# Three of the seven MLP input blocks made on chip, and the causal mask moved into the scan, in a one-layer trunk kernel

## The chip, the cores and the metric

The kernel runs on one core of a Trainium2 chip. Time is device time of one execution in microseconds (us); lower is better. A core has a matrix engine (PE, whose weight loads PEld run beside it), three engines for element work (DVE, ACT, POOL) and a queue engine (SP) that issues loads; stores are issued from POOL's queue. PE works at one of two clocks, which the profile gives as a granted share: 1.0 or 0.5.

## The reference, cut to what matters

One layer, 2048 tokens, width 1024: stick-breaking attention (8 heads of 64), a gated convolution and a spatial gate share one projection; then an MLP of width 4096.

```
h   = rmsnorm(x) * (1 + scale_m) + shift_m
p   = h @ w_in                        # split into q, k, v, conv and gate columns
mix = concat[attention, conv, gate] @ w_out
x   = x + gate_m * mix
h   = rmsnorm(x) * (1 + scale_f) + shift_f
x   = x + gate_f * (relu(h @ w1)**2 @ w2)
out = rmsnorm(x)

# attention, z = q k^T / 8, mask = key < query (strict)
log_stay  = where(mask, log_sigmoid(-z), 0)
log_after = reverse_cumsum(log_stay) - log_stay
w   = where(mask, exp(log_sigmoid(z) + log_after), 0)
out = w @ v
```

## The kernel before

All matrix work is done on numbers split in two parts (`split`: a rounded part by an ACT cast at L127, the remainder by a DVE subtraction at L130), three matmuls for each product.

The program has these stages in time. **Phase 1** (0 to about 713 us) does both halves of 1024 tokens: normalise, project, attention, convolution and gate. Attention is 64 tasks (`attention`): each makes the scores z of two query blocks of 128 against 256 keys each, has them turned into weights by `weights` (three ACT functions, a DVE step, two DVE scans, a copy, a DVE subtraction, an ACT exponential), then transposes and multiplies by v. A matmul of a bf16 mask tile with a bf16 identity (L459) adds a large negative number to the scores that the causal mask forbids. **Output blocks** (713 to about 942) multiply the mix by w_out, first half and then second (the second from about 820); each tile of 512 columns is read from its bank `po` by DVE (`mo`, L769) and stored as rows `x`.

While the second half's output blocks run, the first half's MLP input is prepared in steps that the output loop calls two at a time (`prepare_input`, started by `bg.tick`): load two rows tiles, square sums on ACT (L207), four small DVE steps and two scalings (`x`, L987), transposes on PE into `pt` (L992), shift and scale on ACT into `hf` (L997), store to DRAM (`hd`). Then four passes load pairs of these tiles back (`a1`, `a2`) and DVE makes the sums S1 to S4 (L1011 to L1014), stored to DRAM (`hs`). **Up** (942 to 1600) is a seven-product scheme for the first MLP matrix: products with the key `ababcbc` accumulate in three banks (pa, pb, pc), 16 units for each half of the tokens. Its moving operands are seven blocks of the input, A11, S2, A12, S3, S1, A22, S4 (numbers 0 to 6), each loaded from DRAM by `input` and split into SBUF tiles (h0 to h7 or hx). The second half's input is prepared in the background of the first half's units in the same way. **Down** (1600 to 2216) is the second MLP matrix: its first operands `w` (from DRAM `ar`) and h0 to h7 are split during Up's last products, and its four accumulators py take over Up's banks; the third of them is pc's bank.

Every engine runs its instructions in the order of its queue; that order is fixed when the kernel is built. A load waits for one of six landing buffers, the tiles `hf`, `mo`, `xr` and `hs` share a pool of six.

Of the kernel before, what the change touches and what calls it, by code (L numbers as in the profile page):

```python
# [19 lines left out]
P = 128  # L20
D = 1024
# [63 lines left out]
def trunk(ctx: ExitStack, tc: tile.TileContext, x, c, ada_w, ada_b, norm_mix_g, norm_mlp_g,  # L85
# [224 lines left out]
    with ExitStack() as ph:  # L310
# [86 lines left out]
        identb = ac.tile([P, P], BF16, name="identb")  # L397
        mask = ac.tile([P, 256], BF16, name="mask")
# [4 lines left out]
        def mixer_constants():  # L403

            V.tensor_copy(identb, ident)
            m32 = etile("m32")[:, :256]
            GP.memset(m32, 0.0)
            GP.affine_select(out=m32[:, P:], in_=m32[:, P:], pattern=[[-1, P]],
                             compare_op=ALU.is_gt, fill=NEG, base=0, channel_multiplier=1)
            GP.memset(m32[:, 0:P], NEG)  # L410
            V.tensor_copy(mask, m32)
# [20 lines left out]
        def weights(e, z, lo, init, save):  # L432
# [5 lines left out]
            for a, b in lo:  # L438
                r = e[:, a:b][:, ::-1]
                V.tensor_tensor_scan(r, r, r, init, ALU.add, ALU.bypass)  # L440
            V.tensor_copy(save, e.rearrange("p (b k) -> p b k", b=len(lo))[:, :, 0])
            V.tensor_tensor(e, z, e, ALU.subtract)
            A.activation(e, e, AF.Exp)

        def attention(half, pair, j, gl, qp, qq, kk, vv, a_sb):
# [5 lines left out]
            last = None  # L451
            for b in range(2):
                o = (2 * qp + b) * P
                c0 = 256 * b if first and b == 0 else 256 * b + P
                zb = z[:, b * 256:(b + 1) * 256]
                with tc.issue_after(last.ins) if last is not None else nullcontext():
                    T.matmul(zb, lhsT=qq[:, 0, o:o + P], rhs=kk[:, o:o + 256], start=True, stop=False)
                    T.matmul(zb, lhsT=qq[:, 1, o:o + P], rhs=kk[:, o:o + 256], start=False, stop=False)
                    last = T.matmul(z[:, c0:(b + 1) * 256], lhsT=identb, rhs=mask[:, c0 - 256 * b:256],  # L459
                                    start=False, stop=True)  # L460
            e = etile()
            weights(e, z, ((0, 256), (256, G)), 0.0, carry[:, half, h, ib:ib + 2])
# [451 lines left out]
    class Up:  # L914
# [55 lines left out]

        def prepare_input(self, half):

            for g in range(NG):
                for tp in range(2):
                    xs = []
                    ss = sp.tile([P, 4], F32, name="ss", tag="ss")
                    for b in range(2):
                        t0 = (2 * tp + b) * P
                        t = landing("x")
                        load(out=t, in_=x1d[half * NG + g][t0:t0 + P, :])  # L980
                        xs.append(t)
                    yield
                    for b in range(2):
                        sum_squares(ss[:, b:b + 1], xs[b])
                    r = rstd_of(ss[:, 0:2], 2, 1.0 / D)
                    for b in range(2):
                        V.tensor_scalar_mul(xs[b], xs[b], r[:, b:b + 1])  # L987
                    yield
                    for k in range(0, KT, 2):
                        pt = bank("pt")  # L990
                        for m in range(4):
                            T.transpose(pt[:, m * P:(m + 1) * P],  # L992
                                        xs[m % 2][:, (k + m // 2) * P:(k + m // 2 + 1) * P], ident)
                        f = etile("hf")
                        for m in range(2):
                            sl = slice(m * UC, (m + 1) * UC)
                            A.activation(f[:, sl], pt[:, sl], AF.Identity,  # L997
                                         bias=SH_F[:, k + m:k + m + 1], scale=SC_F[:, k + m:k + m + 1])
# [41 lines left out]
        def inputs_after(self, gl):  # L1040

            if gl == 0:
                bg.finish(self.coming)
                for i in (4, 5, 6, 0, 1):
                    self.input(0, i)
# [296 lines left out]
```

## Time and profile before

| | |
|---|---|
| median of 3 runs | 2219.91 us (2218.26 to 2220.62) |
| profiled execution | 2221.83 us |
| its span | 2220.1 us |
| mean granted PE clock | 0.985 |
| PE busy | 2129.2 us, 96% |
| DVE busy | 1445.0 us, 65% |
| ACT busy | 1013.7 us, 46% |

The span is the time between the first and last instruction of the profiled execution; 1.7 us lie around it. A busy PE is a PE with a matmul under way; matmuls overlap, so what one costs is read from the distance between two starts, not from its own duration.

### The profile page before, as it was taken

To read this page: it belongs to the slowest core of one execution; us is meant where nothing else is said; L and a number is where in the kernel's file an instruction comes from. 1 tells how busy PE (TensorE), PEld (TensorE's weight loads), DVE (VectorE), ACT (ScalarE), POOL (GpSimd) and SP (SyncE) were. 2 spreads that over 40 slices of the span, in tenths; PEclk is the share of its full clock that TensorE was granted. 3 is DMA by queue.
4 is the path that set the end of the run, shared out by engine and by line. 5 is a ranking of instruction groups with operands and counts; after the bars stand their busy time and mean duration, and the time that the engine had idled before them with its cause. 6 is when DMAs were issued, how large, how long until landed. Compare 5 with 4: busy or idle time off the path is not lost. (4 is left out here: it accounts for less than half of the span.)

```text
span 2220.1 us, 30066 instructions
## 1 busy us (share of the span) xinstructions
PE 2129.2 (96%) x11071; PEld 1797.7 (81%) x11071; DVE 1445.0 (65%) x2413; ACT 1013.7 (46%) x1718; POOL 332.0 (15%) x579
## 2 busy tenths in 40 slices
PE   7999999999999988899999999999999999999998
PEld 3887887888788988877888777878788888888886
DVE  4878868767768543776766777778743434347675
ACT  4645647645656234366444644444523323224432
POOL 0021211020211112223322132323200000000000
PEclk9999999999999999999999999999999999999999
DMA  8464544243435466967744687777854435437572
GB/s 304 134 207 115 163 142 131 68 140 88 117 121 162 135 224 233 327 225 244 280 156 154 225 280 256 253 237 248 308 188 153 159 120 165 143 126 231 199 241 86
DMA packets 223216, 415.37 MB, mean 187 GB/s; under 512 B 18400, under 2 KB 106416, under 8 KB 223056
## 3 DMA queue, kind: packets, MB, share of 16 engines
q1 hardware_dynamic: 177424, 264.28, 36.9%
q0 software_dynamic: 45504, 149.00, 19.3%
q8 instruction: 90, 1.47, 0.3%
q14 instruction: 70, 0.57, 0.1%
q10 hardware_dynamic: 128, 0.04, 0.0%
HBM read 262.18 MB, written 142.67 MB: 182 GB/s over the span
## 5 line engine op out<-in xcount | busy, mean ns | idle before, releaser
L1201 PE MATMUL py<-h,w 128*128 128x512 f32 x2688 | 610.7, 389 | 0.0
L1201 PEld LDWEIGHTS py<-h,w 128*128 128x128 f32 x2688 | 504.5, 188 | 105.8 <-issue 1.0
L130 DVE TENSOR_TENSOR w<-ar,w 128x1024 fp32r<-128x1024 f32 x112 | 137.1, 1224 | 263.7 <-ACT w L127 263.3
L127 ACT CAST w<-ar 128x1024 fp32r<-128x1024 f32 x112 | 118.0, 1054 | 370.4 <-PE py L1201 350.4
L127 ACT CAST w<-raw 128x512 fp32r<-128x512 f32 (+1 forms) x215 | 155.1, 736 | 131.4 <-PE pc L1089 48.9
L278 PE MATMUL po<-w,h 128*128 128x256 f32 x1536 | 195.0, 289 | 9.9 <-DVE mo L769 7.3
L130 DVE TENSOR_TENSOR w<-raw,w 128x512 fp32r<-128x512 f32 (+1 forms) x215 | 176.8, 834 | 37.9 <-ACT w L127 36.9
L278 PEld LDWEIGHTS po<-w,h 128*128 128x128 f32 x1536 | 191.4, 197 | 10.7 <-issue 10.0
L1089 PE MATMUL pc<-hx,w 128*128 128x512 f32 x768 | 193.2, 401 | 6.8 <-DVE hid L1063 6.8
L1089 PE MATMUL pa<-h,w 128*128 128x512 f32 x768 | 190.0, 396 | 7.8 <-ACT s L1056 7.8
L1089 PE MATMUL pb<-h,w 128*128 128x512 f32 x768 | 186.7, 391 | 3.6 <-DVE s L1058 3.6
L1089 PEld LDWEIGHTS pc<-hx,w 128*128 128x128 f32 x768 | 145.7, 190 | 42.6 <-DVE hid L1063 8.1
L1089 PEld LDWEIGHTS pa<-h,w 128*128 128x128 f32 x768 | 145.7, 191 | 42.4 <-ACT s L1056 11.2
L1089 PEld LDWEIGHTS pb<-h,w 128*128 128x128 f32 x768 | 143.8, 188 | 35.1 <-DVE s L1058 3.7
L269 PE MATMUL pc<-h,w 128*128 128x512 f32 x576 | 137.4, 394 | 0.0
L269 PEld LDWEIGHTS pc<-h,w 128*128 128x128 f32 x576 | 106.6, 188 | 21.3
L1064 ACT ACTIVATE hid<-hid 128x512 f32<-128x512 f32 x96 | 60.5, 630 | 124.2 <-DVE hid L1063 123.1
L278 PE MATMUL pv<-w,h 128*128 128x256 f32 x768 | 99.5, 285 | 0.0
L1300 POOL DMA_DIRECT2D out_dram<-y x24 | 13.0, 541 | 560.8 <-DVE y L1299 559.6
L1089 PE MATMUL pb<-hx,w 128*128 128x512 f32 x384 | 95.1, 396 | 1.2 <-DVE s L1058 1.2
L278 PEld LDWEIGHTS pv<-w,h 128*128 128x128 f32 x768 | 94.5, 191 | 0.1
L269 PE MATMUL pk<-h,w 128*128 128x512 f32 x384 | 94.1, 398 | 0.1
(215 smaller groups left out, 3285.3 us busy)
## 6 DMA issues: line engine op xcount, KB each, us to landing
ar<-ad SPq DMA_DIRECT2D x112, 512.0 KB, 3.9
ad<-hid POOLq DMA_DIRECT2D x128, 256.0 KB, 3.2
raw<-in_mlp_w_dram SPq DMA_DIRECT2D x62, 512.0 KB, 5.7
ad<-hsum POOLq DMA_DIRECT2D x96, 256.0 KB, 3.2
aw<-in_ada_w_dram SPq DMA_DIRECT2D x32, 512.0 KB, 4.5
f<-in_mlp_w_dram SPq DMA_DIRECT2D x32, 512.0 KB, 4.7
w2s<-f POOLq DMA_DIRECT2D x64, 256.0 KB, 2.9
w<-w2s SPq DMA_DIRECT2D x32, 512.0 KB, 4.5
```

The costliest lines, as they stand in the source:

```text
L127: A.copy(hi, src)
L130: V.tensor_tensor(lo, src, hi.bitcast(F32), ALU.subtract)
L269: T.matmul(ps, lhsT=w[k][:, a, c0:c0 + P], rhs=hT[k][:, b], start=n == 0, stop=n == 3 * KT - 1)
L278: T.matmul(ps, lhsT=hT[k][:, a, tb * P:(tb + 1) * P], rhs=w[k][:, b], start=n == 0, stop=n == 3 * KT - 1)
L1064: A.activation(t, t, AF.Relu)
L1089: T.matmul(ps[key], lhsT=w[:, a, k * P:(k + 1) * P], rhs=h[k // 2][:, b, k % 2], start=start and m == 0, stop=m == 11, skip_group_check=no ...
L1201: T.matmul(ps[tb], lhsT=self.a[q][:, a, u * G + tb * P:u * G + (tb + 1) * P], rhs=self.w[at, c][:, b, u], start=c == 0 and u == 0 and n == ...
L1300: (load if end else store)(out=out2[t0:t0 + P, sl], in_=y)
```

## The change

1. The mask matmuls go, and with them the rule that orders the two query blocks of a task. The scan gets a second operand `restart` (1, and 0 on the diagonal), with which the running sum is multiplied after each addition, so that it starts anew below the diagonal. After the subtraction, a DVE minimum with a tile `cap` (0 and a large negative number) is taken on the 2 x 128 columns of the keys of the query's own block.
2. The first half's S1, S2 and S3 are summed on DVE from the `hf` tiles while they are on chip, and split in place into the hx tiles (`prepare_first`, `sums_first`). A11, A12 and A22 still go through DRAM, and S4 is stored once summed. The half's DMAs: 12 stores of 256 KB into hd in place of 16, 4 into hs in place of 16, no reload of a1 and a2 (8 x 512 KB before), 8 loads of 512 KB of blocks in place of 14.
3. The steps before the transposes are called one by one, with more steps between (`rows_T`); this holds for both halves.
4. Blocks are loaded one step ahead of their splits; blocks 5 and 6 of the first half are split inside Up. The tiles hold other blocks: S2, S3 and S1 in hx, blocks 0, 2, 5 and 6 in h0 to h7. So Down's first operands are prepared after the products 0, 2, 5 and 6 of the last unit, each pair when its tiles are free (before: after 1 to 4).

```diff
-        def weights(e, z, lo, init, save):
+        def weights(e, z, lo, init, save, own=None):
...
                 r = e[:, a:b][:, ::-1]
-                V.tensor_tensor_scan(r, r, r, init, ALU.add, ALU.bypass)
+                if own is None:
+                    V.tensor_tensor_scan(r, r, r, init, ALU.add, ALU.bypass)
+                else:
+                    V.tensor_tensor_scan(r, r, restart[:, ::-1], init, ALU.add, ALU.mult)
...
             V.tensor_tensor(e, z, e, ALU.subtract)
+            if own is not None:
+                V.tensor_tensor(own, own, cap.unsqueeze(1).to_broadcast([P, 2, P]), ALU.min)
             A.activation(e, e, AF.Exp)
...
-                with tc.issue_after(last.ins) if last is not None else nullcontext():
-                    T.matmul(zb, lhsT=qq[:, 0, o:o + P], rhs=kk[:, o:o + 256], start=True, stop=False)
-                    T.matmul(zb, lhsT=qq[:, 1, o:o + P], rhs=kk[:, o:o + 256], start=False, stop=False)
-                    last = T.matmul(z[:, c0:(b + 1) * 256], lhsT=identb, rhs=mask[:, c0 - 256 * b:256],
-                                    start=False, stop=True)
+                for s in range(2):
+                    T.matmul(z[:, b * 256:(b + 1) * 256], lhsT=qq[:, s, o:o + P],
+                             rhs=kk[:, o:o + 256], start=s == 0, stop=s == 1)
...
+        def rows_T(self, half, g, tp, order, tile_):
...
+                load(out=t, in_=x1d[half * NG + g][t0:t0 + P, :])
+                xs.append(t)
+            yield None
+            yield None
+            for b in range(2):
+                sum_squares(ss[:, b:b + 1], xs[b])
+            yield None
+            r = rstd_of(ss[:, 0:2], 2, 1.0 / D)
+            for b in range(2):
+                V.tensor_scalar_mul(xs[b], xs[b], r[:, b:b + 1])
+            yield None
+            yield None
+            for k in order:
...
+        DIRECT = (1, 3, 4)
...
+        def prepare_first(self):
...
+            for tp in range(2):
+                kept = {}
+                for g in range(NG):
+                    order = (0, 4, 2, 6) if g else (0, 2, 4, 6)
+                    for got in self.rows_T(0, g, tp, order, lambda: self.out_tile("hf")):
+                        if got is not None:
+                            k, f = got
+                            kept[g, k] = f
+                            if g == 0 or k >= 4:
+                                self.put_rows(0, g, tp, k, f)
+                            if g == 1 and k >= 4:
+                                yield
+                                yield from self.sums_first(tp, k - 4, kept)
+                        yield
+
+        def sums_first(self, tp, k, kept):
+            a11, a12, a21, a22 = kept[0, k], kept[0, k + 4], kept[1, k], kept[1, k + 4]
+            s1, s2, s4 = (self.xp.tile([P, G], F32, name="s", tag="s", bufs=3) for _ in range(3))
+            V.tensor_tensor(s1, a21, a22, ALU.add)
+            V.tensor_tensor(a21, a11, a21, ALU.subtract)
+            V.tensor_tensor(s2, s1, a11, ALU.subtract)
+            V.tensor_tensor(s4, a12, s2, ALU.subtract)
...
+            store(out=hs[0][3][k:k + 2, :, cols_].rearrange("k p t -> p k t"),
+                  in_=s4.rearrange("p (k t) -> p k t", k=2))
+            for i, t in ((1, s2), (3, a21), (4, s1)):
+                yield
+                o = self.h[0][i][k // 2]
+                split(o[:, 0, :, cols_], o[:, 1, :, cols_], t.rearrange("p (k t) -> p k t", k=2), A)
...
-                if 0 < n - 7 * (NU - 1) <= 7:
-                    self.input(1, n - 7 * (NU - 1) - 1)
+                if n in (1, 3):
+                    if n == 1:
+                        self.loaded.append(self.input_load(0, 6))
+                    self.input_split(0, 5 + n // 2, self.loaded.pop(0))
+                at = n - 7 * (NU - 1)
+                if at == 0:
+                    self.loaded = [self.input_load(1, 0)]
+                if 0 < at <= 7:
+                    if at < 7:
+                        self.loaded.append(self.input_load(1, at))
+                    self.input_split(1, at - 1, self.loaded.pop(0))
                 last = n - self.N + 7
-                if 0 < last <= 4:
-                    down.weights(0, 2 * last - 2)
-                    down.weights(0, 2 * last - 1)
+                if last in (0, 2, 5, 6):
+                    c = 2 * (0, 2, 5, 6).index(last)
+                    down.weights(0, c)
+                    down.weights(0, c + 1)
```

On PE, the first attention task of the program stood like this before (z scores, kk and qq the keys and queries, identb and mask the bf16 tiles):

```order
L457 MATMUL z_1429<-kk_1352,qq_1312 128x256
L458 MATMUL z_1429<-kk_1352,qq_1312 128x256
L459 LDWEIGHTS identb_219
L459 MATMUL z_1429<-mask_220,identb_219 128x256
L457 MATMUL z_1429<-kk_1352,qq_1312 128x256
L458 MATMUL z_1429<-kk_1352,qq_1312 128x256
L459 LDWEIGHTS identb_219
L459 MATMUL z_1429<-mask_220,identb_219 128x128
L278 MATMUL pv_1446<-w_907,h4_552 128x256 x6
```

and stands like this in the changed kernel:

```order
L460 MATMUL z_1427<-kk_1350,qq_1310 128x256 x4
L278 MATMUL pv_1443<-w_905,h4_550 128x256 x6
```

Two mask matmuls and their weight loads are gone from each of the 64 tasks, and nothing has moved between the four score matmuls.

On PE, the first transposes of the preparation stood like this before (pt the transposes' banks, x the scaled rows, po a bank of the output blocks; po_9533 is the first bank of the second half's blocks):

```order
L278 MATMUL po_9533<-w_9384,h2_9312 128x256 x6
L278 MATMUL po_9533<-w_9384,h3_9313 128x256 x6
L992 MATMUL pt_9626<-ident_79,x_9569 128x128
L992 MATMUL pt_9642<-ident_79,x_9569 128x128
L992 MATMUL pt_9655<-ident_79,x_9569 128x128
L992 MATMUL pt_9626<-ident_79,x_9571 128x128
```

and stand like this in the changed kernel, where po_9467 is that first bank and po_9579 the second:

```order
L278 MATMUL po_9467<-w_9318,h3_9247 128x256 x6
L278 MATMUL po_9579<-w_9315,h0_9244 128x256 x6
L278 MATMUL po_9579<-w_9315,h1_9245 128x256 x6
L278 MATMUL po_9579<-w_9318,h2_9246 128x256 x6
L278 MATMUL po_9579<-w_9318,h3_9247 128x256 x6
L278 MATMUL po_9579<-w_9315,h0_9244 128x256 x6
L278 MATMUL po_9579<-w_9315,h1_9245 128x256 x5
L996 MATMUL pt_9604<-ident_79,x_9509 128x128
L996 MATMUL pt_9613<-ident_79,x_9509 128x128
L278 MATMUL po_9579<-w_9315,h1_9245 128x256
```

They stand 35 matmuls of the output blocks later.

On DVE, in the second half's output blocks, the sums of the first half's blocks stood like this before (hs the sums, a1 and a2 the tiles loaded back, mo the reading of an output bank po, w a split of Up's first weights):

```order
L1011 TENSOR_TENSOR hs_10196<-a1_10151,a2_10152 128x512
L1012 TENSOR_TENSOR hs_10197<-hs_10196,a1_10151 128x512
L1013 TENSOR_TENSOR hs_10198<-a1_10151 128x512
L1014 TENSOR_TENSOR hs_10199<-a2_10152,hs_10197 128x512
L130 TENSOR_TENSOR w_10307<-raw_10165,w_10307 128x1024
L130 TENSOR_TENSOR w_10310<-raw_10167,w_10310 128x1024
L1011 TENSOR_TENSOR hs_10236<-a1_10208,a2_10209 128x512
L1012 TENSOR_TENSOR hs_10237<-hs_10236,a1_10208 128x512
L1013 TENSOR_TENSOR hs_10238<-a1_10208 128x512
L1014 TENSOR_TENSOR hs_10239<-a2_10209,hs_10237 128x512
L769 TENSOR_TENSOR mo_10248<-po_10171,gate_bc_85 128x512
```

and the first of the four passes stands like this in the changed kernel (L771 and L773 are the lines of mo now, s the sums):

```order
L1044 TENSOR_TENSOR s_9788<-hf_9749,hf_9784 128x512
L1045 TENSOR_TENSOR hf_9749<-hf_9609,hf_9749 128x512
L1046 TENSOR_TENSOR s_9789<-s_9788,hf_9609 128x512
L771 TENSOR_TENSOR mo_9824<-po_9754,gate_bc_85 128x512
L1047 TENSOR_TENSOR s_9790<-hf_9651,s_9789 128x512
L130 TENSOR_TENSOR hx_9502<-s_9789,hx_9502 128x2x256
L130 TENSOR_TENSOR hx_9504<-hf_9749,hx_9504 128x2x256
L773 TENSOR_TENSOR mo_9824<-mo_9824,xr_9752 128x512
L130 TENSOR_TENSOR hx_9506<-s_9788,hx_9506 128x2x256
```

The last two passes before stood in one piece ahead of a reading of a bank; now readings stand between the sums of a pass, the sums read tiles that ACT made and not loaded ones, and three half-width splits follow each pass. Between the transposes and the scaling of the next rows, one place is different too: two splits of Up's weights stand ahead of the third scaling,

```order
L196 TENSOR_SCALAR v_9984<-ss_9947 128x2
L130 TENSOR_TENSOR w_9996<-raw_9830,w_9996 128x1024
L771 TENSOR_TENSOR mo_9980<-po_9920,gate_bc_85 128x512
L199 TENSOR_TENSOR t_9986<-r_9985 128x2
L130 TENSOR_TENSOR w_9999<-raw_9832,w_9999 128x1024
L773 TENSOR_TENSOR mo_9980<-mo_9980,xr_9918 128x512
L200 TENSOR_TENSOR t_9986<-t_9986,v_9984 128x2
L201 TENSOR_SCALAR t_9986<-t_9986 128x2
L202 TENSOR_TENSOR r_9985<-r_9985,t_9986 128x2
L990 TENSOR_SCALAR x_9948<-x_9948,r_9985 128x1024
```

where before they stood behind the last of them.

On DVE, at the end of Up, the reading of the last product's bank pc (the second `hid<-pc`) stood like this before (hid the activations, hsum their sums, room a piece of modulation work, w and h splits of Down's operands):

```order
L130 TENSOR_TENSOR h6_16083<-w2_16081,h6_16083 128x1024
L130 TENSOR_TENSOR h7_16088<-w2_16086,h7_16088 128x1024
L130 TENSOR_TENSOR w_16093<-ar_16091,w_16093 128x1024
L1063 TENSOR_TENSOR hid_16096<-pc_16068,s_16066 128x512
L1063 TENSOR_TENSOR hid_16121<-pb_15984,s_15982 128x512
L130 TENSOR_TENSOR w_16147<-ar_16145,w_16147 128x1024
L1070 TENSOR_TENSOR hsum_16125<-hid_16121,hid_16096 128x512
L365 TENSOR_SCALAR room_16166<-aw_16203,cact_160 128x512
L1070 TENSOR_TENSOR hsum_16128<-hsum_16125,hid_16040 128x512
L1125 TENSOR_TENSOR hid_16121<-hid_16040,hid_16121 128x512
L1063 TENSOR_TENSOR hid_16150<-pc_16068,s_16007 128x512
```

and stands like this in the changed kernel:

```order
L1132 TENSOR_TENSOR hid_15974<-pc_15956,s_15954 128x512
L130 TENSOR_TENSOR h4_16001<-w2_15999,h4_16001 128x1024
L1132 TENSOR_TENSOR hid_16009<-pb_15892,s_15890 128x512
L130 TENSOR_TENSOR h5_16006<-w2_16004,h5_16006 128x1024
L130 TENSOR_TENSOR w_16045<-ar_16043,w_16045 128x1024
L130 TENSOR_TENSOR h6_16035<-w2_16033,h6_16035 128x1024
L1139 TENSOR_TENSOR hsum_16013<-hid_16009,hid_15974 128x512
L130 TENSOR_TENSOR h7_16040<-w2_16038,h7_16040 128x1024
L1139 TENSOR_TENSOR hsum_16016<-hsum_16013,hid_15938 128x512
L1204 TENSOR_TENSOR hid_16009<-hid_15938,hid_16009 128x512
L1132 TENSOR_TENSOR hid_16048<-pc_15956,s_15905 128x512
```

Four splits (h4 to h7) have come to stand between the first reading of pc and the second. On ACT, the casts that belong to them stand in this order in the changed kernel:

```order
L127 CAST h5_16006<-w2_16004 128x1024
L127 CAST w_16045<-ar_16043 128x1024
L1133 ACTIVATE hid_16009<-hid_16009 128x512
L127 CAST h6_16035<-w2_16033 128x1024
L1134 ACTIVATE hid_16009<-hid_16009 128x512
L127 CAST h7_16040<-w2_16038 128x1024
L1133 ACTIVATE hid_16048<-hid_16048 128x512
```

The tiles h4 to h7 hold blocks 5 and 6 of Up now, so the cast of h5 can't start before the sixth of the last unit's seven products has ended, and that of h7 not before the seventh.

## Rows read from the trace of the kernel before

**Rows 1.** The page: busy time, share of the span and instructions of each engine.
```profile
PE 2129.2 (96%) x11071; PEld 1797.7 (81%) x11071; DVE 1445.0 (65%) x2413; ACT 1013.7 (46%) x1718; POOL 332.0 (15%) x579
```
**Rows 2.** Busy time by stage (start:end length, busy us of each engine, clock, DMA, GB/s).
```profile
0.00:713.00 713.00, 673.45 (x3964) 573.14 (x3964) 522.25 (x1029) 406.56 (x744) 97.42 (x167) 0.98 0.47 144
...
820.00:942.00 122.00, 103.11 (x803) 101.39 (x802) 63.32 (x102) 45.19 (x80) 30.83 (x47) 0.92 0.84 285
942.00:1250.00 308.00, 301.75 (x1333) 245.14 (x1332) 215.07 (x353) 164.50 (x299) 77.05 (x136) 0.99 0.58 205
1250.00:1600.00 350.00, 334.76 (x1421) 268.83 (x1420) 269.34 (x405) 172.18 (x283) 97.70 (x182) 0.99 0.77 265
```
**Rows 3.** What PE waited for from 820 to 945 (us, times, longest).
```profile
PE pt L992 <- DVE x L987: 11.1, 4, 4.7
PE po L278 <- DVE mo L769: 7.3, 1, 7.3
```
**Rows 4.** PE from 818 to 910 (start, us, work, [idle before <-releaser]).
```profile
826.75 2.79 PE L992 MATMUL pt<-ident,x 128*128 128x128 f32 x12 [4.67 <-DVE x L987]
...
839.40 0.43 PE L992 MATMUL pt<-ident,x 128*128 128x128 f32 x2 [2.66 <-DVE x L987]
...
850.65 0.30 PE L992 MATMUL pt<-ident,x 128*128 128x128 f32 x1 [3.51 <-DVE x L987]
...
868.58 29.05 PE L278 MATMUL po<-w,h 128*128 128x256 f32 x240 [0.26 <-ACT hf L997]
904.93 5.33 PE L278 MATMUL po<-w,h 128*128 128x256 f32 x24 [7.30 <-DVE mo L769]
```
**Rows 5.** DVE from 884 to 906.
```profile
900.96 0.69 DVE L1012 TENSOR_TENSOR hs<-hs,a 128x512 f32<-128x512 f32 x1 [1.37 <-DMA hs<-hs]
...
904.09 0.69 DVE L769 TENSOR_TENSOR mo<-po,gate_bc 128x512 f32<-128x512 f32 x1 [0.41 <-DMA hs<-hs]
```
**Rows 6.** Two short stretches, columns as in rows 2.
```profile
826.50:831.50 5.00, 4.75 (x22) 4.45 (x23) 2.06 (x4) 2.85 (x6) 1.68 (x3) 0.50 0.67 230
...
899.70:909.90 10.20, 4.97 (x23) 5.00 (x24) 7.08 (x10) 1.04 (x1) 3.61 (x6) 0.50 0.90 309
```
**Rows 7.** PE in one attention task, from 309.7 to 311.
```profile
310.10 0.36 PE L457 MATMUL z<-kk,qq 128*128 128x256 f32 x1
310.30 0.28 PE L458 MATMUL z<-kk,qq 128*128 128x256 f32 x1
310.43 0.23 PE L459 MATMUL z<-mask,identb 128*128 128x128 bf16 x1
310.46 0.36 PE L457 MATMUL z<-kk,qq 128*128 128x256 f32 x1
```
**Rows 8.** The mask matmuls as a group (count, busy us, mean ns).
```profile
L459 PE MATMUL z<-mask,identb 128*128 128x128 bf16 x120 | 27.6, 230 | 0.0
```
**Rows 9.** Groups of DVE in phase 1 (count, busy us, mean ns).
```profile
L440 DVE TENSOR_TENSOR_SCAN e<-e 128x256 f32<-128x256 f32 x122 | 77.8, 676 | 1.1
...
L442 DVE TENSOR_TENSOR e<-z,e 128x512 f32<-128x512 f32 x60 | 41.1, 686 | 1.4
...
L659 DVE TENSOR_TENSOR gu<-gu,mx 128x128 f32<-128x128 f32 x32 | 8.9, 278 | 0.1
```
**Rows 10.** What PE waited for from 945 to 1250.
```profile
PE pt L992 <- DVE x L987: 2.1, 3, 1.4
```
**Rows 11.** PE from 1594 to 1604: the last product of Up.
```profile
1597.11 3.06 PE L1089 MATMUL pc<-hx,w 128*128 128x512 f32 x12 [1.13 <-DVE hid L1063]
```
**Rows 12.** The page's groups: a split's two steps, and an activation.
```profile
L130 DVE TENSOR_TENSOR w<-ar,w 128x1024 fp32r<-128x1024 f32 x112 | 137.1, 1224 | 263.7 <-ACT w L127 263.3
L127 ACT CAST w<-ar 128x1024 fp32r<-128x1024 f32 x112 | 118.0, 1054 | 370.4 <-PE py L1201 350.4
...
L1064 ACT ACTIVATE hid<-hid 128x512 f32<-128x512 f32 x96 | 60.5, 630 | 124.2 <-DVE hid L1063 123.1
```
**Rows 13.** DVE from 1594 to 1606: the second reading of pc.
```profile
1601.81 0.68 DVE L1063 TENSOR_TENSOR hid<-pc,s 128x512 f32<-128x512 f32 x1
```

More of the change, by code (lines that the diff above doesn't have):

```diff
@@ L1 @@
-from contextlib import ExitStack, nullcontext
+from contextlib import ExitStack
 import concourse.bass as bass
@@ L395, in mod_rows @@
                 yield
-        identb = ac.tile([P, P], BF16, name="identb")
-        mask = ac.tile([P, 256], BF16, name="mask")
+        restart = ac.tile([P, 256], F32, name="restart")
+        cap = ac.tile([P, P], F32, name="cap")
         swT = ac.tile([P, 2, 4 * P], F32R, name="swT")
@@ new lines, in put_rows, with place @@
+        def put_rows(self, half, g, tp, k, f):
+            t0 = g * G + tp * UC
+            store(out=hd[half][k:k + 2, :, t0:t0 + UC].rearrange("k p t -> p k t"),
+                  in_=f.rearrange("p (k t) -> p k t", k=2))
+        DIRECT = (1, 3, 4)
+        def place(self, i):
+            if i in self.DIRECT:
+                n = 2 * self.DIRECT.index(i)
+                return [self.xp.tile([P, 2, 2, G], F32R, name="hx", tag=f"hx{n + j}")
+                        for j in range(2)]
+            n = 2 * (0, 2, 5, 6).index(i)
+            return [htile(n + j) for j in range(2)]
@@ new lines, in prepare_first @@
+        def prepare_first(self):
+            for i in self.DIRECT:
+                self.h[0][i] = self.place(i)
+            for tp in range(2):
[12 more added lines that the diff above has]
+                        yield
@@ L974, in prepare_input @@
                 for tp in range(2):
[L975 to L998, printed above, removed]
-                        t0 = g * G + tp * UC
-                        store(out=hd[half][k:k + 2, :, t0:t0 + UC].rearrange("k p t -> p k t"),
-                              in_=f.rearrange("p (k t) -> p k t", k=2))
+                    for got in self.rows_T(half, g, tp, range(0, KT, 2), lambda: etile("hf")):
+                        if got is not None:
+                            self.put_rows(half, g, tp, *got)
                         yield
@@ L1016, in prepare_input, with input_load @@
                     store(out=hs[half][j][k], in_=e[j])
-        def input(self, half, i):
-            tiles = []
+        def input_load(self, half, i):
+            raws = []
             for j in range(2):
@@ L1031, in input, with input_split, first_inputs @@
                 load(out=raw, in_=src.rearrange("k p t -> p k t"))
-                if i < 4:
-                    t = htile(2 * i + j)
-                else:
-                    t = self.xp.tile([P, 2, 2, G], F32R, name="hx", tag=f"hx{2 * i + j}")
-                split(t[:, 0], t[:, 1], raw, A)
-                tiles.append(t)
-            self.h[half][i] = tiles
+                raws.append(raw)
+            return raws
+        def input_split(self, half, i, raws):
+            tiles = self.h[half][i] = self.place(i)
+            for t, raw in zip(tiles, raws):
+                split(t[:, 0], t[:, 1], raw, A)
+        def first_inputs(self):
+            raws = self.input_load(0, 0)
+            yield
+            for i, after in ((0, 2), (2, 5)):
+                ahead = self.input_load(0, after)
+                for _ in range(3):
+                    yield
+                self.input_split(0, i, raws)
+                raws = ahead
+            self.loaded = [raws]
         def inputs_after(self, gl):
+            bg.finish(self.coming)
             if gl == 0:
-                bg.finish(self.coming)
-                for i in (4, 5, 6, 0, 1):
-                    self.input(0, i)
-            else:
-                for i in (2, 3):
-                    self.input(0, i)
+                self.coming = bg.now(self.first_inputs())
         def out_tile(self, name):
```

35 lines of the change are left out of this document (24 added, 11 removed).

## The prediction

> **What bounds the kernel now.** I read the page first, then busy time by stage, then PE's waits and timeline in the stages that the change touches, and last the other engines' timelines around the longest waits. PE is busy 96% of the span, DVE 65% [rows 1], so the kernel is as long as PE's work plus the stretches in which PE waits or runs at half clock. In phase 1 PE is idle for 713.0 - 673.45 = 39.6 us, spread over many short waits; in the second output stage for 122.0 - 103.1 = 18.9 us, with a mean granted clock of 0.92 where phase 1 has 0.98; in the two parts of Up for 6.3 and 15.2 us [rows 2]. So there are two things to win: PE work taken away, and the waits of the output stage.
>
> Nearly all of those 18.9 us are four waits [rows 3, 4]: three times the transposes of the preparation wait for the scaled rows (4.67, 2.66, 3.51 us), once the output matmuls wait 7.30 us for a bank to be read. The reading came late because it stands on DVE behind the sums hs, which wait for stores of earlier sums to free their tiles: at 900.96 and just before 904.09 the releaser is the store of hs [rows 5]. The DMA engines are 84% busy in this stage [rows 2]. After two of the waits the trace shows PE at half clock, from 826.5 to 831.5 and from 899.7 to 909.9, with 4.75 and 4.97 us of PE work in them [rows 6]; done at full clock that is half as long, so another 4.9 us were lost. Together the stage loses 23.8 us.
>
> **Masks.** In one attention task the first score matmul of the second block starts 0.36 us after that of the first [rows 7]. Plain matmuls of the same shape follow each other at 29.05 / 240 = 0.121 us [rows 4], so two of them should take 0.242, and the mask with its weight load takes 0.118. The group's mean duration, 230 ns [rows 8], would give 0.230, but those durations overlap: the distance counts. 64 tasks x 2 x 0.118 = -15.1 us. The Trainium skill ("TensorE: Matmul & The Clock Gate", section "Back-to-back issue gap") states about 81 ns per matmul for a sustained stream of pairs of weight load and 128-column matmul. By this figure the masks would be worth an estimated 10.4 us and the sum below -25; the distance of rows 7 speaks against it, and I go by the rows.
>
> What the change adds for it is 64 minimums on DVE. The trace has none of 256 columns of this form; DVE takes 0.278 us for 128 columns and 0.686 for 512 [rows 9], so on a line between them 0.41 us for 256, or 26 us of DVE in all. The bounds are the two rows, 18 to 44 us. DVE has 522 us of work in 713 [rows 2]; it will have 548 in some 700. The minimum also stands in each task's chain from scores to transposes, making it 0.4 us longer; PE has other tasks' matmuls in between. It costs nothing where that cover holds. It does not hold everywhere: PE's 39.6 us of waits in this stage are such places. Per task DVE goes from 8.2 to 8.6 us and PE from 10.5 to 10.3, so I let the waits grow by 3 us (bounds 0 and 10, the latter about 0.4 us for 24 of the 64 tasks). The scan's second operand is priced at nothing: the scan named two operands before, and at 0.676 us for 256 columns it takes 2.6 ns a column, where a subtraction that reads two tiles takes 0.686 for 512, or 1.3 ns [rows 9]; the reading isn't what limits it. Phase 1: -12 us, from -5 to -15.
>
> **Output stage.** The sums no longer wait for reloads or for stores of four tiles; they read tiles that ACT has just made, and of the sums S4 alone is stored; there are 16 of them as before. In MB, 4 hd and 12 hs stores of 256 KB, 8 reloads and 6 block loads of 512 KB go, about 11 MB of the 35 MB that 285 GB/s over 122 us make [rows 2]. The mechanism of the 7.30 us wait is therefore gone, and with it its 2.5 us of half clock: -9.8. The new order shows three DVE readings of banks between the sums and splits of the first pass where before two passes and two wide splits stood ahead of one. Nothing as long as 7 us can gather on DVE without DMA waits: four sums (0.69 each) and three half splits are 4.8 us, and a reading stands inside them.
>
> The first transposes stand 35 output matmuls later: 35 x 0.121 = 4.2 us of the 4.67 us wait are filled, and the 2.4 us of half clock behind it go too. The second and third wait (2.66 and 3.51) come from the same steps, where ACT's square sums and DVE's scaling were asked for one step ahead of the transposes; there are two more steps there now. But two wide splits stand ahead of the third scaling: 2 x 1.22 us of DVE [rows 12], fed by two casts of 1.05. That leaves an estimated 1 to 2 us of wait at this place; about 0.5 at the first, 0 to 2 at the fourth. I keep 4 us of the 23.8 in all: -20 us. Bounds: -12 (the 7.30 with its clock and 2 us more), -24 (all).
>
> **Up.** The same longer steps serve the second half's rows: three waits of 2.1 us in total [rows 10], of which I take 2 off: -2 (0 to -4). Blocks 5 and 6 are split within the first unit, their loads a step earlier; the first wait there stays about as it was: 0 +- 1. Loading the second half's blocks a step ahead does not change the order of splits on ACT and DVE: 0 +- 4, the latter a fourth of the 15.2 us of waits in that part.
>
> **Up to Down: a new wait.** Down's third accumulator uses pc's bank, so PE can start it only when DVE has read the last product. Call T the end of that product. The first two accumulators take 12 matmuls, as many as the last product, which ran 3.06 us from its first start to its last end [rows 11]; starts alone are a little closer, so PE wants the bank at about T + 2.8. In the new order that reading stands behind four splits, whose casts must wait for Up's last products because they write into their tiles. ACT from the end of the sixth product (T - 2.8): h5, w, an activation, h6, an activation, h7, or 4 x 1.05 + 2 x 0.63 = 5.5 us [rows 12], so T + 2.7. DVE behind it: a split of 1.22, two sums and the reading, each 0.69 or 0.68 [rows 9, 13]: T + 2.7 + 1.22 + 3 x 0.69 = T + 6.0, and one more combination at 0.69 if the sums weren't done before it: no more than T + 6.7. PE waits 3.2 to 3.9 us, and may lose up to 1.7 at half clock behind it, as after the waits of 3.5 us. Before, PE waited 1.13 us ahead of the last product [rows 11], and the last reading at 1601.81 [rows 13] came in time. That 1.13 wait hung on a split's operand from DRAM and may go or stay. I take +4, bounds 0 and +10 (a late load of `ar` would stand ahead of all of it).
>
> **Sum.** -12 - 20 - 2 + 4 = -30 us from the profiled 2221.83 gives 2192. The median of the runs is 1.9 us lower; measured against it, the same sum would be 2190. I say 2191.
>
> **The rivals.** (a) *DVE gives the mask's time back.* If phase 1's waits grow by nearly as much as the masks save, because the minimum lengthens chains that PE waits for, phase 1 gains 0 to -4: 2201. For it: 39.6 us of waits that name DVE and ACT again and again. Against it: the average task has 1.7 us of room on DVE. (b) *The output stage's waits move.* The preparation still needs the same transposes, square sums and scalings on three engines, now with 12 more half-width splits in the same stage; if waits of 3 us stay at three places with their clock, the stage gains 10: 2201. For it: ACT and DVE queues hold the splits of Up's weights ahead of a scaling. Against it: the stage's DVE is busy only 63 of 122 us [rows 2]. Both together: 2211. (c) *Slower than before.* The minimum reads a tile that is spread over the second dimension and a strided output; should such a form run several times slower than the two plain forms [rows 9], DVE becomes the bound of phase 1. DVE does 522 / 64 = 8.2 us for each task, PE 10.3 without masks. From a minimum of 2.1 us on DVE would set the pace, and at 2.7 us (64 x 0.6 = 38 us more than PE's pace) all that the other parts give is gone: 2228. No group of DVE that I read comes near six times the linear price. (d) *The change doesn't do what it says* in that the DMA time saved was hidden: true of most of it, since only the 7.3 us hung on it; that is in the sum.
>
> **Chances.** My forecast with its own bounds (2182 to 2198): 0.62; (a) 0.13; (b) 0.14; both 0.05; (c) 0.02; the rest, among it a gain beyond the sum, 0.04. 8 in 10 are held by 2180 to 2208. About 4.4 us (0.2%) is what a measurement can tell from no change. Faster by more than that means under 2215.5: 0.94; the same 0.03; slower 0.03.
>
> **What would show it.** The profile of after should have no 7 us wait of output matmuls for a reading, a stage of about 102 to 107 us in place of 122 with a clock near 1.0; no matmul of a mask, phase 1 shorter by about 12 us, a DVE group of 64 minimums of about 0.41 us; a PE wait of 3 to 5 us at the third accumulator of Down. I am wrong if the minimum takes over 1 us, if waits of over 3 us for x or a bank remain in the output stage, or if phase 1 is within 5 us of its old length.

## The result and the profile after

The changed kernel takes 2195.86 us in the median of 4 runs (2191.99 to 2200.36) against 2219.09 of 4 runs before (2217.15 to 2220.62): ratio 0.9897, 95% interval 0.9874 to 0.9919. Run again beside the experiments it gave 2195.75 (6 runs, ratio 0.9898, 0.9878 to 0.9918). Forecast were 2191 and 2180 to 2208. The profiled execution is the 2191.99 one, 29.8 us under that of before, of which the places below are taken. It is the fastest of its four runs, and that of before (2221.83) lies above its own median; the medians are 23.2 us apart.

The page's busy times of the changed kernel, to set beside [rows 1]:

```profile
PE 2109.1 (96%) x10943; PEld 1784.0 (81%) x10943; DVE 1466.5 (67%) x2481; ACT 1014.1 (46%) x1724; POOL 324.8 (15%) x564
```

PE has 128 matmuls less, DVE 21 us more work; PE's share of the span is what it was, so work and waits both shrank. Busy time in the changed kernel's output stage (columns as in [rows 2]; the stage begins at another time, and the row ends 17 us after Up's start):

```profile
812.00:930.00 118.00, 115.97 (x899) 112.07 (x899) 81.78 (x135) 59.43 (x108) 24.17 (x34) 1.00 0.74 246
```

Where the 29.8 us came from follows from the start of each stage's first matmul in the two profiles:

| stretch | before | after | change | forecast |
|---|---|---|---|---|
| start to first output matmul | 713.5 | 707.1 | -6.4 | -12 (phase 1) |
| first output half | 102.7 | 103.8 | +1.1 | in phase 1 |
| second output half, to Up | 125.6 | 101.9 | -23.7 | -20 |
| Up, units 1 to 15 of the first half | 306.2 | 306.7 | +0.5 | -2 |
| Up, the rest to the last unit | 331.3 | 326.1 | -5.2 | 0 +- 4 |
| last unit and Down | 640.8 | 644.7 | +4.0 | +4 |

**Output stage.** PE's waits from 812 to 930 in the changed kernel are one row, against the 18.4 us of [rows 3]; no output matmul waits for a reading any more:

```profile
PE pt L996 <- DVE x L990: 1.9, 2, 1.4
```

Its timeline has both, and between them every transpose is in time:

```profile
822.43 0.41 PE L996 MATMUL pt<-ident,x 128*128 128x128 f32 x2 [1.43 <-DVE x L990]
...
856.40 0.30 PE L996 MATMUL pt<-ident,x 128*128 128x128 f32 x1 [0.46 <-DVE x L990]
...
878.16 34.80 PE L278 MATMUL po<-w,h 128*128 128x256 f32 x288
```

Against [rows 4]: 1.43 us stands where 4.67 stood, the second and fourth group of transposes don't wait, the third waits 0.46 behind the two splits, and 288 output matmuls run without a break where the 7.30 us wait was.

**Up to Down.** The forecast new wait is there. PE and DVE of the changed kernel around it:

```profile
1564.89 2.88 PE L1280 MATMUL py<-h,w 128*128 128x512 f32 x12
1570.92 9.36 PE L1280 MATMUL py<-h,w 128*128 128x512 f32 x33 [3.15 <-DVE hid L1132]
```
```profile
1567.85 1.22 DVE L130 TENSOR_TENSOR h<-w,h 128x1024 fp32r<-128x1024 f32 x1
1568.98 0.68 DVE L1139 TENSOR_TENSOR hsum<-hsum,hid 128x512 f32<-128x512 f32 x1
1569.59 0.68 DVE L1204 TENSOR_TENSOR hid<-hid 128x512 f32<-128x512 f32 x1
1570.19 0.68 DVE L1132 TENSOR_TENSOR hid<-pc,s 128x512 f32<-128x512 f32 x1
```

The split of h7, two sums and the reading end at 1570.87; PE goes on at 1570.92, 6.0 us after the start of Down's first accumulator, and at half clock until 1574.5.

**Phase 1.** The minimum costs what the line between the two rows of [rows 9] gave; a row of the changed kernel's DVE:

```profile
L448 DVE TENSOR_TENSOR e<-e,cap 128x256 f32<-128x256 f32 x60 | 25.2, 420 | 1.1
```

Phase 1 gave less than forecast, and the price of the masks is not the reason. In the changed kernel the scores of one task and what follows them are

```profile
706.52 0.72 PE L460 MATMUL z<-kk,qq 128*128 128x256 f32 x4
707.08 1.12 PE L278 MATMUL po<-w,h 128*128 128x256 f32 x8
```

0.56 us from the first score matmul to the first of other work. The task of [rows 7] began at 310.10, and other work after it here:

```profile
310.83 0.48 PE L269 MATMUL pc<-h,w 128*128 128x512 f32 x1
```

0.73 us. The difference is 0.17 us for two masks, but the starts behind that one differ by more. Medians over the 51 tasks of each profile with no gap and no half clock behind them, in us from the first score matmul:

| start of other work | before | after | difference |
|---|---|---|---|
| its first matmul | 0.724 | 0.555 | 0.169 |
| its second | 1.035 | 0.785 | 0.250 |
| its third | 1.264 | 1.017 | 0.247 |
| its fourth | 1.499 | 1.248 | 0.251 |

From the second start on the difference stays at 0.25 us, so a mask with its weight load costs 0.125 us, close to the 0.118 of the forecast, and the 64 tasks 16 us. Two thirds of a mask's price are paid behind it: the next start follows the mask after 0.04 us, but the matmul after it, be it a score matmul or other work, then takes 0.08 us longer until the next start than it does without a mask ahead.

### The profile page after: what moved, and what is told of

Its sections match the earlier page's. It is cut to its first block, busy times and chain, and to the rows that moved or that the text cites. A ratio compares the mean times of both kernels' runs of the same rounds, so it can differ in the third digit from the quotient of the medians.

```text
span 2190.3 us, 29799 instructions
## 1 busy us (share of the span) xinstructions
PE 2109.1 (96%) x10943; PEld 1784.0 (81%) x10943; DVE 1466.5 (67%) x2481; ACT 1014.1 (46%) x1724; POOL 324.8 (15%) x564
## 5 line engine op out<-in xcount | busy, mean ns | idle before, releaser
L1158 PE MATMUL pb<-hx,w 128*128 128x512 f32 x768 | 192.7, 400 | 6.2 <-DVE s L1127 6.0
L278 PE MATMUL po<-w,h 128*128 128x256 f32 x1536 | 190.2, 285 | 2.0 <-PEq L683 2.0
L278 PEld LDWEIGHTS po<-w,h 128*128 128x128 f32 x1536 | 186.9, 193 | 2.2 <-issue 2.2
L1158 PEld LDWEIGHTS pb<-hx,w 128*128 128x128 f32 x768 | 145.1, 190 | 41.6 <-DVE s L1127 7.4
L269 PE MATMUL pc<-h,w 128*128 128x512 f32 x576 | 135.5, 391 | 0.0
L1158 PE MATMUL pb<-h,w 128*128 128x512 f32 x384 | 95.0, 397 | 4.2 <-DVE s L1127 4.2
L1158 PE MATMUL pc<-hx,w 128*128 128x512 f32 x384 | 95.3, 397 | 0.0
L1158 PE MATMUL pc<-h,w 128*128 128x512 f32 x384 | 92.8, 390 | 2.1 <-DVE hid L1132 2.1
```

The costliest lines, as they stand in the source:

```text
L269: T.matmul(ps, lhsT=w[k][:, a, c0:c0 + P], rhs=hT[k][:, b], start=n == 0, stop=n == 3 * KT - 1)
L278: T.matmul(ps, lhsT=hT[k][:, a, tb * P:(tb + 1) * P], rhs=w[k][:, b], start=n == 0, stop=n == 3 * KT - 1)
L1158: T.matmul(ps[key], lhsT=w[:, a, k * P:(k + 1) * P], rhs=h[k // 2][:, b, k % 2], start=start and m == 0, stop=m == 11, skip_group_check=no ...
```

## The experiments

Phase 1 is compared below by one length that leaves out the start-up, where the profiles differ by up to 5 us: from the first `pu` matmul to the first output matmul. It is 680.6 us before and 677.3 in the changed kernel's profile. The two stretches of these kernels, before first:

```profile
32.90:713.50 680.60, 655.71 (x3916) 566.01 (x3916) 508.21 (x997) 395.05 (x726) 96.72 (x161) 0.99 0.44 134
```
```profile
29.80:707.10 677.30, 645.34 (x3792) 558.93 (x3793) 527.00 (x1053) 394.32 (x724) 96.21 (x158) 0.98 0.45 136
```

PE is busy 10.4 us less and idle 7.1 us more, and 23.9 us of the stretch are at half clock where before has 17.1. The rows differ by 124 matmuls, the masks of 62 tasks, so some 15.5 us of PE's work are gone from a stretch that is 3.3 us shorter.

### Part 1 alone, part 1 undone

The first is the kernel before with the masks' part of the change; the second is the changed kernel with that part taken back. The line of the scan stands for the part, whose other lines are those of the change above:

```diff
...
-                V.tensor_tensor_scan(r, r, r, init, ALU.add, ALU.bypass)
...
+                    V.tensor_tensor_scan(r, r, restart[:, ::-1], init, ALU.add, ALU.mult)
...
```

> The kernel before with part 1 alone (no mask matmuls, restart in the scan, one minimum a task). In the changed kernel the first output matmul came 6.4 us earlier (707.1 against 713.5), where the masks' PE work is 15.1. Theory A (the minimum lengthens waits of phase 1): first output matmul at 706 to 709, the output stage unchanged at 125 us, whole time 5 to 7 us under before. Rival B (something of the preparation reaches back into phase 1): first output matmul at 698 to 701, whole time 12 to 15 us under before.

> The changed kernel with part 1 undone (masks back, no restart, no minimum). Theory A, parts add up: first output matmul at 713 to 714, second output stage 102 us in place of 125.6 to Up's start, the wait at the third accumulator of Down 3 us; whole time 18 to 24 us under before. Rival: the preparation's gain depends on the faster phase 1 (loads and splits arrive at other times): 10 us or less.

Part 1 alone: 2213.62 us (12 runs), ratio 0.9974, 0.9960 to 0.9988; first output matmul at 707.5, output stage 125.8. The preparation and the rest alone: 2197.44 us (6 runs), ratio 0.9907, 0.9888 to 0.9926; output stage 102.3, the same wait of 3.15 us at Down. Its first output matmul came at 711.4, earlier than expected, because phase 1 began 2.7 us earlier in this profile; phase 1 itself has its old length. The parts add up within the noise (0.9974 x 0.9907 = 0.988, where the whole change has 0.990), and what phase 1 falls short belongs to part 1.

### The minimum twice, the minimum not at all

```diff
                 V.tensor_tensor(own, own, cap.unsqueeze(1).to_broadcast([P, 2, P]), ALU.min)
+                V.tensor_tensor(own, own, cap.unsqueeze(1).to_broadcast([P, 2, P]), ALU.min)
```

> The changed kernel with the minimum taken twice in each task (the same result; 64 more DVE steps of 0.42 us, 27 us). Theory A: phase 1 waits for DVE in the places where it does now, and grows by 5 to 12 us: first output matmul at 712 to 719, whole time 5 to 12 us over the changed kernel. Rival B (the minimum is covered, the lost gain has another cause): within 2 us of the changed kernel.

The other one gives the same weights without a minimum: the running sum starts at 1e30 behind the last key, so that forbidden keys have a huge sum, and is set to nothing at the key below the diagonal (column 127 + query of 256).

```diff
-                    V.tensor_tensor_scan(r, r, restart[:, ::-1], init, ALU.add, ALU.mult)
+                    V.tensor_tensor_scan(r, restart[:, ::-1], r, 1.0e30, ALU.mult, ALU.add)
...
-                V.tensor_tensor(own, own, cap.unsqueeze(1).to_broadcast([P, 2, P]), ALU.min)
```

> The changed kernel without the minimum: the scan starts from 1e30 at the far end and is multiplied by 0 before the addition at the key below the diagonal, so the forbidden keys' weights vanish in the exponential by themselves. No PE instruction differs. Theory A: DVE loses 25 us in phase 1 and each task's chain 0.4 us, first output matmul 5 to 9 us earlier (698 to 702), whole time 5 to 9 us under the changed kernel. Rival B: within 2 us of it.

Two minimums: 2201.51 us (6 runs), ratio 0.9922, 0.9903 to 0.9940; none: 2187.08 us (5 runs), ratio 0.9849, 0.9826 to 0.9872. In phase 1:

| kernel | length | DVE busy in it | PE idle in it | at half clock |
|---|---|---|---|---|
| before; part 1 undone | 680.6; 681.2 | 508; 509 | 25; 27 | 17; 17 |
| the five profiles with one minimum | 674.5 to 679.4, mean 676.7 | 526 to 527 | 32 | 16 to 31 |
| two minimums | 682.1 | 548 | 37 | 24 |
| seeded scan (three profiles) | 673.4, 672.4, 673.0 | 506 to 507 | 31 to 33 | 17 to 24 |

The rows of two minimums and of the seeded scan, to set beside the two at the head of this section:

```profile
30.20:712.30 682.10, 644.67 (x3792) 557.68 (x3793) 548.46 (x1113) 393.72 (x724) 96.08 (x158) 0.98 0.44 135
```
```profile
30.60:704.00 673.40, 640.89 (x3791) 556.55 (x3792) 506.44 (x994) 395.33 (x725) 96.13 (x158) 0.98 0.45 137
```

In the whole time theory A holds: two minimums cost 5.8 us over the changed kernel, and none gains 8.7 (by the medians; by the ratios to before 5 and 11). The first output matmul came at 712.3 with two, as expected, and at 704.0 with none, later than the 698 to 702. Phase 1 is 3.7 us shorter without the minimum, and 5.4 longer with a second one (one profile, where the five with one minimum spread over 4.9), each for 20 to 22 us of DVE work. So the minimum is not covered.

The second minimum is seen as waits, 5 us more of PE's idle time. The first is not: idle time is the same with one and with none. It counts only gaps beyond the end of a matmul, and these ends are modelled. An estimate that needs no ends takes each distance from one start to the next less the lower quartile of the same sequence of four matmuls over all traces at full clock. It puts waits and half clock together at 42 us with the masks, 50 to 55 with one minimum, 59 with two and 46 to 48 with the seeded scan.

Most of what phase 1 falls short is not the minimum's. Without any, on a DVE that does no more than before, phase 1 keeps 7.9 us (680.9 to 673.0) of the masks' 15.5, about half; the other half came back as waits and half clock. PE's waits that grew are for DVE's tiles of the same chain: the products' for `a_sb` from 0.8 to 3.4 us, the transposes' for `wT` from 3.7 to 5.2. That PE, with less to do, reaches the same results sooner would explain it, but no run here tests it. Nor does phase 1 show more than 3.7 of the 8.7 us between the times of the seeded and the changed kernel; where the rest lies stays open.

### Down's last splits behind the reading

On DVE, the remainders of h6 and h7 are put behind the reading of the last product.

```diff
-            V.tensor_tensor(t, ps, s, ALU.add)
+            self.reading = V.tensor_tensor(t, ps, s, ALU.add)
...
-                if last in (0, 2, 5, 6):
-                    c = 2 * (0, 2, 5, 6).index(last)
+                if last in (0, 2, 5):
+                    c = 2 * (0, 2, 5).index(last)
...
+                if last == 6:
+                    with tc.issue_after(self.reading.ins):
+                        down.weights(0, 6)
+                        down.weights(0, 7)
```

> The changed kernel once more, as the measure for the runs beside it: 2192 to 2200 us, ratio to before 0.988 to 0.991.

> The changed kernel with the last two of Down's splits (h6, h7) put behind the reading of the last product's bank on DVE. Theory A (the wait at Down's third accumulator is the queue of DVE): the reading comes 2.4 us earlier, the wait falls from 3.15 us to under 1 and its half clock goes, 3 to 5 us under the changed kernel. Rival (the reading waits for ACT or the load of w in any order, or h6 and h7 are then late for Down): within 1 us of it, or a wait of the same length some 16 us later.

2194.42 us (6 runs), ratio 0.9895, 0.9872 to 0.9919, beside 2195.75 of the changed kernel: not told apart by the times. The traces tell it: the first 24 products of Down (of 12 matmuls each) take 68.3 us in all five profiles with this edit, here and below, and 71.1 to 72.4 in the six profiles that have the new preparation without it; no later wait stands against it.

```profile
1575.15 2.11 PE L1284 MATMUL py<-h,w 128*128 128x512 f32 x8 [1.79 <-DVE hid L1132]
```

The wait is 1.79 us, and no half clock follows. So DVE's queue made 1.4 us of it; the expected fall to under 1 us was too much, because the reading still stands behind the split of `w`, three sums and a piece of modulation work.

### Both together

> The scan that starts from 1e30 without a minimum, and the late h6 and h7 together. If the two gains are independent: 10 to 14 us under the changed kernel, 2180 to 2184 us. If they are not: no better than the first alone (2187).

> The seeded scan with late h6 and h7 once more, as the measure for the two runs beside it: 2184 to 2189 us.

2186.44 us (4 runs, ratio 0.9855, 0.9828 to 0.9881) and 2186.47 (4 runs, 0.9859, 0.9834 to 0.9884): 9 us under the changed kernel, less than the 10 to 14 expected, and no more than the seeded scan alone within what the times can tell. The 3 us at Down are in both traces. The seeded scan carries the gain; no version tried is shown to be faster.

### More steps ahead of the second half's sums

In the changed kernel PE waits 5.3 us in Up near 1065, with half clock behind it, because DVE waits for a reload of the second half's rows ahead of a sum; PE and DVE there:

```profile
1070.40 2.07 PE L1158 MATMUL pb<-hx,w 128*128 128x512 f32 x4 [5.31 <-DVE s L1127]
```
```profile
1062.44 0.69 DVE L1072 TENSOR_TENSOR hs<-a,a 128x512 f32<-128x512 f32 x1 [5.20 <-DMA a<-hd]
```

```diff
-                yield
-                yield
+                for _ in range(4):
+                    yield
```

> The changed kernel with two more steps between the reloads of the second half's blocks and their sums inside Up (four in place of two). In the changed kernel DVE waits 5.2 us there for a reload, and PE 5.3 us for DVE with 2.4 us of half clock behind it, near 1065. Theory A (the sums are asked for too early): that wait falls below 2 us, 4 to 8 us under the changed kernel. Rival (the reload itself is late because the DMA engines are full, and stays ahead of the same DVE work): the wait moves by a few products and stays within 2 us of its size.

2195.66 us (6 runs, ratio 0.9898, 0.9877 to 0.9918): no gain. The wait went into three, of 1.31, 2.86 and 1.48 us, 5.65 in all. Theory A falls: the sums are late wherever they are asked for, as the rival has it, though not for the reload alone. DVE now waits 5.4 us for a store of earlier sums, until 1057, and 3.6 us for a reload, until 1078. The DMA engines' share is 0.93 from 1040 to 1070 in the changed kernel's trace; whether that alone makes reloads and stores late was not tried.

### More cover for a task's chain

On the seeded kernel with late h6 and h7, one step is added ahead of the product with v, or ahead of the transposes:

```diff
             split(wT[:, 0], wT[:, 1], wt, A)
             yield
+            yield
             av = pw.tile([P, 256], F32, name="av", tag="av")
```
```diff
+            yield
             yield
             yield
             wt = pw.tile([P, G], F32, name="wt", tag="wt")
```

> The same with one more step between the split of a task's weights and their product with v. Of the masks' 15.1 us phase 1 kept 8 in the seeded kernel; PE's idle time there rose from 26 to 32 us, in waits of the products and transposes for wT and a_sb. Theory C (the chain of a task is too short of cover on PE): the waits for wT fall by 3 us or more, phase 1 is 2 to 5 us shorter. Rival D (the waits are for DVE's queue as such, wherever the task's steps stand): within 1.5 us, other waits in place of these.

> The same with one more step between a task's scores and its transposes. Theory C: phase 1 is 2 to 5 us shorter. Rival D: within 1.5 us, or longer since a score bank is held longer (two of them) and the next task's scores wait.

2194.81 us (5 runs, ratio 0.9887, 0.9866 to 0.9909) and 2187.43 (6 runs, 0.9864, 0.9840 to 0.9888), phase 1 at 681.6 and 674.6 us, beside 2186.47 and 673.0. PE's longest group of waits in phase 1, in the first of the two, then in the kernel without added steps:

```profile
PE wt L462 <- DVE wT L130: 19.5, 20, 3.6
```
```profile
PE wt L462 <- DVE wT L130: 5.2, 7, 2.0
```

In the first, the products with v no longer wait for wT, but the transposes of the next task now wait for the one bank `wt`, which DVE reads for wT, and phase 1 is 8.6 us longer: neither expectation had that. Theory C falls. Of rival D it holds that other waits take the place of these; its 1.5 us fit the second edit (1.6 us longer) and not the first. Whether a second bank `wt` would help was not tried.

### The masks twice

```diff
+                    T.matmul(z[:, c0:(b + 1) * 256], lhsT=identb, rhs=mask[:, c0 - 256 * b:256],
+                             start=False, stop=False)
                     last = T.matmul(z[:, c0:(b + 1) * 256], lhsT=identb, rhs=mask[:, c0 - 256 * b:256],
```

> The kernel before with each mask matmul and its weight load issued twice (the forbidden scores get the large negative number twice, which changes no weight). In the kernel before one block of a task takes 0.36 us between first starts, 0.118 of it put down to the mask. If that is its price: 0.47 to 0.48 us with two, 15 us more PE work in phase 1; if a streamed one costs 0.08 us: 0.44 us and 10 us more. How much of that the time shows tells how much of a mask's price is covered by waits: theory (half of it, as when they were removed): 6 to 10 us over before; rival (waits absorb no added work): 13 to 16 us over before.

2230.12 us (6 runs), ratio 1.0052, 1.0032 to 1.0072; phase 1 691.5 us. One block of a task with two masks:

```profile
311.99 0.36 PE L457 MATMUL z<-kk,qq 128*128 128x256 f32 x1
312.19 0.28 PE L458 MATMUL z<-kk,qq 128*128 128x256 f32 x1
312.31 0.23 PE L459 MATMUL z<-mask,identb 128*128 128x128 bf16 x1
312.38 0.22 PE L461 MATMUL z<-mask,identb 128*128 128x128 bf16 x1
312.41 0.37 PE L457 MATMUL z<-kk,qq 128*128 128x256 f32 x1
```

From first start to first start it takes 0.42 us where [rows 7] have 0.36: the second mask costs 0.06 us (medians over 57 tasks: 0.839 us for a task, 0.724 before, so 0.058, and the starts behind differ by no more), less than either expectation. That is 7.4 us of PE work. Phase 1 grew by more, 10.9 us in this one profile: idle time by 2.6, and 20.5 us of it are at half clock where before has 17.1. The runs are 11.5 us over before (7 to 16), between the two expectations. So there is no sign that waits absorb added PE work, though they gave back only half of what was taken away. The price of a mask depends on its neighbours: 0.058 behind another mask, 0.125 between matmuls of another type.

## Why the prediction was right, and where its sizes were off

**Masks: the price held.** 0.118 us was taken for a mask with its weight load. The task with and without masks differs by 0.25 us, so 0.125 for a mask and 16 us in all, where 15.1 were forecast. The Trainium skill's 81 ns in "TensorE: Matmul & The Clock Gate", section "Back-to-back issue gap", is for a sustained stream of such pairs and would have given 10.4 us. No run here has such a stream: a mask between other matmuls took 0.125 us and one behind another mask 0.058, so the prediction was right to go by its rows.

**The minimum: price right, growth of the waits mis-sized.** 0.420 us was measured where 0.41 was taken. The step that failed is "I let the waits grow by 3 us (bounds 0 and 10)". Phase 1 kept 4.2 us (680.9 to 676.7) of the 15.5 us of masks in it, where 12 were forecast; so 11.3 came back as waits and half clock, past the upper bound. The reason given was too narrow as well: the waits were to grow by the minimum, but the runs put 3.7 us on it, and 7.6 are lost without any minimum. This is rival (a) at its edge, and one of the prediction's own signs of being wrong came true, phase 1 within 5 us of its old length: it is 3.3 us shorter in the profile, and the other 3.1 of the 6.4 us at the first output matmul are an earlier start. The scan with a second operand costs nothing, as priced: 676 ns before, 676 and 677 after.

**Output stage: right in mechanism and a little low.** It gave 23.7 us (22.2 to 23.9 in the other profiles with this preparation), where 20 was forecast. The count of 23.8 had missed a third stretch at half clock, 851.9 to 855.4 before, worth 1.7 us; of the true 25.5, 1.8 are left. The first wait left 1.43 us where 0.5 was expected, the third 0.46 where 1 to 2 were; the fourth was nothing. Rival (b) did not happen: DVE has 82 us of work in 118, its readings still come in time, and none of the waits that the trace shows in its queue there names a DMA, where before some 21 us of them did.

**Up.** The rows' three waits of 2.1 us are gone, yet the stage is 0.5 us longer. DVE waits 5.2 us for a reload ahead of a sum where it waited 4.6, and PE behind it 5.3 us in place of 2.3, with half clock after it both times. Up's first wait of 1.2 us, which I had left as it was, is gone too. The -5.2 us behind unit 15 is no effect of the change that can be shown: the kernel with part 1 alone, which has none of the new preparation, takes 324 us there, the changed kernel 326 and 327, the one with more steps 335, the one before 331. Such waits for loads differ between executions, and the spread of the runs of one kernel (2192 to 2200) is of this size.

**Up to Down: right.** A wait of 3.2 to 3.9 us was forecast at the third accumulator, 3.15 came; the reading was to end at T + 6.0, and it ended 5.8 us after the modelled end of the last product at 1565.06. The sum of +4 was met at 4.0: the first 24 products of Down take 5.0 us longer, wait and half clock, and the 1.1 us wait ahead of the last product is gone. That DVE's queue is the cause is shown in part: two splits less in it took 1.4 us of the wait away, and the half clock behind it.

In sum the forecast was 4 to 5 us low: phase 1 gave 8 us less, the output stage 3 to 4 more. That the total came so near is in part luck, as these errors have opposite signs. The 29.8 us between the two profiles, which match the sum of -30, hold the 5.2 us of Up that can't be shown to be the change's.

## What to carry to other kernels

Price an instruction that is to go by the distance over its whole group, with and without it or with it doubled, and follow the starts behind the group until the difference stays: the first start showed 0.17 us for two masks, the second 0.25. Work taken from the busiest engine is not time won: half of the masks' 15.5 us came back as waits and half clock, with no more work on any other engine. And an engine with 20% of its time free isn't cover: 20 us more work on DVE cost 4 to 5 us of phase 1. Look whether a step can be folded into one that is there already; the seeded scan does what a minimum did, for nothing, and gave more than any of the new places in a queue that the experiments tried.

## What was not expected of the hardware

The same bf16 mask matmul of 128 columns with its weight load costs 0.125 us of PE's time between fp32 score matmuls, and a second one behind it 0.058. Two thirds of the 0.125 are not between the mask and the next start but between the two starts after it. Transposes ahead of score matmuls, which are in both kernels, do the same: behind them the second score matmul starts 0.20 us after the first (medians over 37 and 39 places), behind those of `pv` and `pc` 0.12 us (10 and 9 places). So most groups of four take 0.555 us from their start to the next work and a few 0.467.
